# A deeper ring for the down projection's weight tiles: eight places, loads three column pairs ahead

## The chip, the cores and the metric

The kernel runs on one core of a Trainium2 chip, as one launch. The metric is the device time in microseconds, the median of several runs; lower is better. The engines are called by the names that the profile gives them: PE (TensorE), DVE (VectorE), ACT (ScalarE), SP (SyncE, which issues nearly all DMA transfers here). Each engine works through its own queue in order, and the order in every queue is fixed when the kernel is built: a scheduler of the framework simulates the program and, whenever an engine falls free, gives it the ready instruction of the best priority. `tc.high_priority(n)` treats an instruction as if it stood n instructions earlier in the program.

## The reference

One step of a hybrid decoder layer for a prompt (512 tokens behind 16 meta tokens) and eight sample tokens, all in float32 with `D_MODEL` 2048 and `D_FF` 5632: layer norm, one input projection, sliding-window attention beside causal pooling, output projection, layer norm, a SwiGLU feed-forward and a last layer norm. The part that matters here is the end:

```python
def post_sublayers(h, attn_out, pool_out, w_o, ln1_g, ln1_b, w_gate, w_up, w_down, ln2_g, ln2_b):
    mix = jnp.einsum('bte,ed->btd', jnp.concatenate([attn_out, pool_out], -1), w_o)
    h1 = layer_norm(DEEPNORM_ALPHA * h + mix, ln1_g, ln1_b)
    a = jax.nn.silu(jnp.einsum('btd,df->btf', h1, w_gate)) * jnp.einsum('btd,df->btf', h1, w_up)
    ff = jnp.einsum('btf,fd->btd', a, w_down)
    return layer_norm(DEEPNORM_ALPHA * h1 + ff, ln2_g, ln2_b)
```

## The kernel before

**Products.** Each float32 product is made of three matmuls on rounded halves (`products`, lines 188 to 195): high part by high part, high by low, low by high. A weight tile is therefore first split (`split`, lines 181 to 187): ACT casts it into the high part `wh` (line 185), DVE subtracts to get the low part `wl` (line 186). In the down projection `wh` and `wl` have rings of four tiles each, so the cast for a product waits until PE has finished the product four before it. Gate, up and down projections use a seven-product scheme for 2x2 blocks (Strassen's, in Winograd's form): seven block products instead of eight, with some additions of weight tiles (DVE) and of results.

**The down projection** is the stage from about 1470 to 1954 us. Its reduction has 44 tiles of 128. Forty of them go through the seven-product scheme in four chunks `c` of ten (five pairs, `KP = 5`), the other four ("plain", `PLAIN`) through ordinary products in the stage that follows. For each chunk there are eight column pairs `j` (an output tile j and j+8). So the stage works through 32 pairs, `pairs[x]` with x from 0 to 31. `column_pair(c, j)` is a generator that makes the seven products in the order 1, 7, 2, 6, 4, 5, 3, with 5 x 3 = 15 matmuls each. Products 7, 6, 5 and 3 first need an addition of weight tiles in place (`add`, line 1162, 128x640 on DVE, at high priority); results are added from PSUM (`tri`, two sets of three banks) to the accumulators by DVE in lines 1169, 1174, 1179 and 1182, once each per pair. The loop interleaves two pairs: product 1 of pair x, then the last product (3) of pair x-1, then the rest of pair x.

**Loads.** `load_w(c, j)` (lines 1128 to 1141) loads the weights of a pair as two tiles of 640 KB, `r=0` and `r=1`, by SP (line 1135); for the first chunk also the accumulators' start values (line 1141). `A[0, *]` lie in the tile `r=0`, `A[1, *]` in `r=1`. The first addition of a pair, for product 7, writes `A[1, 0]` and needs both tiles. The last read of `r=0` is the split for product 3, which takes `A[0, 1]`; the last read of `r=1` is the split for product 4, which takes `A[1, 1]`. The tiles rotate through the ring `wd`, which has five places of 1280 columns: two and a half pairs. The loop calls `load_w` for the next pair, x+1, after product 3 of pair x-1. `load_ops` (line 1124) loads the other operands of the products, 260 KB each, for the following chunk. The helper `step(sync)` keeps the steps of these loads in SP's queue in program order; within one step the order is free.

**Around it.** The regions `fr`, `rr` and `mid_*` are large SBUF tiles in which the kernel hands out places by column number; the framework makes every load wait for the readers of the bytes that it overwrites. `pl` (line 1245) holds the weights of the plain tiles for four output tiles at a time, 2048 columns; it has one place of its own during the down projection, and a second is added behind it (line 1258). `af` (line 1215) takes the plain activations from `a_d` through two places. After the down projection come the plain products (`down`, lines 1242 to 1255), the transposes and the last layer norm (`Rows`).

Of the kernel before, what the change touches and what calls it, by code (L numbers as in the profile page):

```python
# [7 lines left out]
F32 = mybir.dt.float32  # L8
# [5 lines left out]
P = 128  # L14
# [8 lines left out]
NTOK = NS + SEQ  # L23
# [36 lines left out]
KP = 5  # L60
# [6 lines left out]
def hybrid_step(ctx, tc, xin, w_in, w_o, w_g, w_u, w_d, w_pool, par_d, cst_d, ident_d, ln2gb, kct_d, vc_d, hist_d,  # L67
# [63 lines left out]
    fr, rr = Region("fr", F32, FRW), Region("rr", F32R, RRW)  # L131
# [25 lines left out]
    @contextmanager  # L157
    def step(*engines):

        block = nc.cur_bb.bb  # L160
        last = block.instructions[-1]
        yield
        code = block.instructions
        start = next(k for k in reversed(range(len(code))) if code[k] is last) + 1
        new = {}
        for i in code[start:]:
            if i.engine in [e.engine for e in engines]:
                new.setdefault(i.engine, []).append(i)
                for j in behind.get(i.engine, ()):
                    tc.add_manual_dep(i, j, mybir.DependencyInfo(mybir.DependencyClass.NoSync,  # L170
                                                                 mybir.DependencyReason.DATA), reason="step")
        behind.update({e: [i.name for i in v][-12:] for e, v in new.items()})
# [8 lines left out]
    def split(s, name, lo=None):  # L181

        wh, wl = [sp[0].tile(list(s.shape), F32R, tag=t, bufs=sp[1]) for t in ("wh", "wl")]
        with tc.high_priority(prio[0]):
            nc.scalar.copy(wh, s)  # L185
            (lo or nc.vector).tensor_sub(wl, s, wh.bitcast(F32))  # L186
        return wh, wl
# [56 lines left out]
    with ExitStack() as sa:  # L244
# [235 lines left out]
        for i in range(2):  # L480
            z = zkv[2 + i]
# [311 lines left out]
    pb, gp = Pool(fr), Pool(rr, Region("mid_b", F32R, MDW))  # L793
# [3 lines left out]
    def bank(name, w=HN):  # L797
        return ps.tile([P, 512], F32, tag="bank", name=name, bufs=banks)[:, :w]

    def slot(name, shape=(2, HN), at=None):  # L800
        return gp.tile([P, *shape], F32R, tag="g", name=name, bufs=NG, at=at)
# [268 lines left out]
    for j, s in enumerate(sets[NKEEP:NKEEP + NFILL]):  # L1070
        if j % 2 == 0:
            f = pb.tile([P, 2, HN], F32, tag="fill", name=f"fill{j}", bufs=NF)
# [27 lines left out]
    accp, rp, pb = Pool(fr), Pool(fr), Pool(fr)  # L1100
    low = fr.take(4 * 1280)
    accp.ring("acc", 2 * NTOK, F32, 8)
    up = [fr.take(1280) for _ in range(3)]
    fr.give(low, 4 * 1280)
    rp.rings["wd"] = [[(fr, x) for x in up + [fr.take(1280) for _ in range(2)]], 1280, 0]
    plp = Pool(fr)
    plp.ring("pl", 2048, F32, 1)
    acc4 = []


# [3 lines left out]
    ops, wd, given = [{n: [] for n in ORDER} for _ in range(NCH)], {}, [0]  # L1114

    def load_ops(c, k):

        for n in ORDER:
            while k and len(ops[c][n]) < KP:
                i = WINO[c][len(ops[c][n])]  # L1120
                t = slot(f"op{c}_{n}_{i}", at=free[given[0] % NG])
                given[0] += 1
                with step(sync):
                    nc.sync.dma_start(t.bitcast(F32), t_d[i, {1: 0, 2: 1, 3: 2, 5: 3, 6: 4, 7: 5, 4: 6}[n]])
                ops[c][n].append(t)
                k -= 1

    def load_w(c, j):
        if c == NCH:
            return  # L1130
        with step(sync):
            for r in range(2):
                raw = rp.tile([P, 2 * KP * P], F32, tag="wd", name=f"wd{c}_{j}_{r}", bufs=5)
                o = P * (c % 2)
                nc.sync.dma_start(raw, w_d[c, j + 8 * r, :, o:o + 2 * KP * P])
                v = raw.rearrange("p (k b c) -> p b k c", k=KP, b=2)
                wd[c, j, r, 0], wd[c, j, r, 1] = v[:, 0], v[:, 1]
            if c == 0:
                acc4.append(accp.tile([P, 4, HN], F32, tag="acc", name=f"acc{j}", bufs=8))
                for r in range(2):  # L1140
                    nc.sync.dma_start(acc4[j][:, 2 * r:2 * r + 2, :].rearrange("p a c -> p (a c)"), h1_d[j + 8 - 8 * r])

    def column_pair(c, j):

        A = {(r, b): wd[c, j, r, b] for r in range(2) for b in range(2)}
        tri = ps.tile([P, 3, 512], F32, tag="tri", name=f"tri{c}_{j}", bufs=2)[:, :, :HN]
        ga, de, al = [tri[:, i, :] for i in range(3)]
        ac = acc4[j]
        if c == 0:
            for r in range(2):  # L1150
                h = ac[:, 2 * r:2 * r + 2, :]
                nc.scalar.activation(h, h, AF.Copy, scale=ALPHA)

        def prod(n, bk, src, first=True):
            wh, wl = split(src, f"d{c}_{j}_{n}")
            for k in range(KP):
                hi, lo = ops[c][n][k][:, 0, :], ops[c][n][k][:, 1, :]
                products([bk], wh[:, k, :], wl[:, k, :], [hi], [lo], k == 0 and first, k == KP - 1, True)

        def add(t, a, b, op):  # L1160
            with tc.high_priority(prio[0]):
                op(A[t], A[a], A[b])  # L1162
            return A[t]


        prod(1, al, A[0, 0])
        yield
        prod(7, ga, add((1, 0), (0, 0), (1, 0), nc.vector.tensor_sub))
        nc.vector.tensor_add(ac[:, 1:3, :], ac[:, 1:3, :], tri[:, 0::2, :])
        yield  # L1170
        prod(2, de, A[0, 1])
        yield
        prod(6, al, add((1, 0), (1, 1), (1, 0), nc.vector.tensor_sub), False)
        nc.vector.tensor_add(ac[:, 0, :], ac[:, 0, :], al)
        yield
        prod(4, ga, A[1, 1], False)
        yield
        prod(5, al, add((0, 0), (1, 0), (0, 0), nc.vector.tensor_add), False)
        nc.vector.tensor_add(ac[:, 0:2, :], ac[:, 0:2, :], tri[:, 0::2, :])  # L1179
        yield  # L1180
        prod(3, al, add((0, 1), (0, 1), (1, 0), nc.vector.tensor_sub), False)
        nc.vector.tensor_add(ac[:, 2:4, :], ac[:, 2:4, :], tri[:, 1:3, :])
        yield
# [3 lines left out]
    load_ops(0, 10)  # L1187
    load_w(0, 1)
    load_ops(0, 25)
    pairs = [(c, j) for c in range(NCH) for j in range(8)]  # L1190
    g, before = [column_pair(0, j) for j in range(2)]
    for i in range(6):
        next(g)
        next(before)
    next(g)
    load_w(0, 2)
    for x, (c, j) in enumerate(pairs[2:], 2):
        g = column_pair(c, j)
        next(g)
        next(before)  # L1200
        if x + 1 < len(pairs):
            load_w(*pairs[x + 1])
        for i in range(5):
            next(g)
            if c + 1 < NCH:

                if j < 7 and i == 0:
                    load_ops(c + 1, 3 if c else 5 if j == 6 else 4)
                elif j == 7:
                    load_ops(c + 1, (4, 0, 5, 0, 5)[i])  # L1210
            elif j == 0 and i == 0:

                ah, al_ = [], []
                for f in range(2 * len(PLAIN)):
                    t = pb.tile([P, NTOK], F32, tag="af", name=f"af{f}", bufs=2)
                    with step(sync):
                        nc.sync.dma_start(t, a_d[f])
                    ah.append(slot(f"ah{f}", (NTOK,), 8 + 2 * f))
                    al_.append(slot(f"al{f}", (NTOK,), 9 + 2 * f))
                    nc.scalar.copy(ah[f], t)  # L1220
                    nc.vector.tensor_sub(al_[f], t, ah[f].bitcast(F32))
        before = g
# [4 lines left out]
    scope.close()  # L1227
    ps, banks = ctx.enter_context(tc.tile_pool(name="psD", bufs=8, space=PS)), 8
    rp.close()
    pb.close()  # L1230
    pb, zp = Pool(fr), Pool(Region("mid_c", F32, MDW))
    places = [x for i in PLAIN for x in PLAIN[i]]
    pw, ws = {}, {}
# [8 lines left out]
    def down(h, m):  # L1242

        if m % 4 == 0 and h == 0:
            pw[h] = plp.tile([P, 4, 4, P], F32, tag="pl", name=f"pl{h}_{m}", bufs=len(plp.rings["pl"][0]))
            for f, (c, x) in enumerate(places):
                nc.sync.dma_start(pw[h][:, :, f, :], w_d[c, m:m + 4, :, x * P:(x + 1) * P].rearrange("m p c -> p m c"))
        hs = DHALF[h]
        out = bank(f"d{h}_{m}", hs.stop - hs.start)
        if h == 0:  # L1250
            ws[m] = split(pw[h][:, m % 4], f"dp{m}")
        wh, wl = ws[m]
        for f in range(4):
            products([out], wh[:, f, :], wl[:, f, :], [ah[f][:, hs]], [al_[f][:, hs]], f == 0, f == 3)
        nc.vector.tensor_add(acc[m][:, hs], acc[m][:, hs], out)

    gb = [[pb.tile([P, 512], F32, name=f"gb{i}_{q}") for q in range(4)] for i in range(2)]
    plp.rings["pl"][0].append((fr, fr.take(2048)))
    gb_loads = [(i, q) for i in range(2) for q in range(4)]

    class Rows:
# [124 lines left out]
```

## Time and profile before

| | |
|---|---|
| time, median of 3 runs | 2029.87 us (2023.43 to 2036.59) |
| the profiled execution's own time | 2030.44 us |
| its span, first to last instruction | 2028.7 us |
| mean granted clock of PE | 0.986 |
| busy: PE, DVE, ACT | 95%, 76%, 47% |
| DMA | 319.27 MB, mean 157 GB/s |

How to read it: times are microseconds from the span's start. A matmul counts as busy for about 0.28 us, while in a dense row one starts every 0.12 us, so a busy share of PE hides short stops; the distance between starts shows them. In the timeline a row has the start, the duration, engine, line, operation, output and inputs, and in brackets the idle time in front of it with what ended it. In the list of waits a row says who waited for whom, for how long in total, how often, and the longest. In a table by stretches each engine has its busy time and count of instructions, and the last three columns are PE's granted clock, the DMA share and GB/s.

### The profile page before, as it was taken

What the parts mean: (1) busy time and instruction counts of PE and PEld (TensorE: products, weight loads), DVE (VectorE), ACT (ScalarE), POOL (GpSimd) and SP (SyncE); (2) the same over time, 40 slices, a digit from 0 to 9 for tenths busy, and PEclk for the clock granted to TensorE, in tenths of its full rate; (3) what the DMA queues carried; (4) which work ended last, traced back from release to release, by engine and by line L of the source; (5) the groups of instructions that cost most, each with busy time, mean ns of one, the idle gap of its engine ahead of it and who ended that gap; (6) DMA issues with size and microseconds to landing.
All of it is one profiled execution on the core that took longest, in us unless ns stands there. A gap on an engine that the chain in (4) does not pass through costs nothing.

```text
span 2028.7 us, 39453 instructions
## 1 busy us (share of the span) xinstructions
PE 1934.3 (95%) x15571; PEld 1889.3 (93%) x15571; DVE 1532.7 (76%) x2730; ACT 946.8 (47%) x1805; POOL 2.5 (0%) x8
## 2 busy tenths in 40 slices
PE   8999999999999999999999999999998889898895
PEld 8999999999989999999999999999998888888895
DVE  6665667667678899888888888888776776767768
ACT  6643436445555445555555555555543333333331
POOL 0000000000000000000000000000000000000000
PEclk9999998999999999999999999999999999999998
DMA  8622223665554555454444444445675535453232
GB/s 261 225 94 70 71 80 97 204 199 183 199 176 163 168 178 168 147 166 138 152 147 156 148 149 150 147 158 168 221 285 190 203 126 201 150 190 119 76 89 85
DMA packets 144986, 319.27 MB, mean 157 GB/s; under 512 B 14160, under 2 KB 65944, under 8 KB 144696
## 3 DMA queue, kind: packets, MB, share of 16 engines
q1 hardware_dynamic: 143680, 314.65, 46.5%
q8 instruction: 122, 2.00, 0.4%
q10 hardware_dynamic: 1120, 2.10, 0.3%
q14 instruction: 64, 0.52, 0.1%
HBM read 265.20 MB, written 54.03 MB: 157 GB/s over the span
## 4 chain that ended last, share of the span: by engine, by line
PE 75%; DMA 10%; DVE 9%; issue 3%; ACT 2%; SPq 0%; DVEq 0%; ACTq 0%
PE p_u L195 6%; PE p_u L192 6%; PE p_u L193 6%; DMA fr<-in_w_d_dram 6%; PE p_g L192 5%; PE p_g L193 5%; PE p_g L195 5%; DVE rr L186 4%; PE tri L195 4%; PE tri L192 4%; PE tri L193 3%; PE o L192 3%; PE o L195 3%; PE o L193 3%; DMA fr<-in_w_u_dram 2%
## 5 line engine op out<-in xcount | busy, mean ns | idle before, releaser
L185 ACT CAST rr<-fr 128x512 fp32r<-128x512 f32 (+1 forms) x1056 | 664.3, 643 | 833.0 <-PE tri L193 211.0
L186 DVE TENSOR_TENSOR rr<-fr,rr 128x512 fp32r<-128x512 f32 (+1 forms) x1056 | 733.9, 715 | 203.9 <-ACT rr L185 198.0
L930 DVE TENSOR_TENSOR fr<-fr 128x1024 f32<-128x1024 f32 x176 | 215.1, 1223 | 61.9 <-DMA fr<-in_w_g_dram 31.5
L192 PE MATMUL p_g<-rr 128*128 128x260 f32 x800 | 226.8, 285 | 7.1 <-DVE fr L1001 6.9
L195 PE MATMUL tri<-rr 128*128 128x260 f32 x696 | 202.6, 291 | 28.8 <-DVE rr L186 27.0
L192 PE MATMUL p_u<-rr 128*128 128x260 f32 x800 | 225.8, 283 | 1.8 <-ACT rr L185 1.0
L195 PE MATMUL p_g<-rr 128*128 128x260 f32 x800 | 222.1, 282 | 1.5 <-DVE rr L186 1.5
L195 PE MATMUL p_u<-rr 128*128 128x260 f32 x800 | 222.2, 282 | 0.0
L193 PE MATMUL p_u<-rr 128*128 128x260 f32 x768 | 215.9, 282 | 0.0
L193 PE MATMUL p_g<-rr 128*128 128x260 f32 x768 | 215.8, 282 | 0.0
L192 PE MATMUL tri<-rr 128*128 128x260 f32 x696 | 201.0, 289 | 4.8 <-DVE fr L1179 3.4
L193 PE MATMUL tri<-rr 128*128 128x260 f32 x696 | 199.0, 286 | 0.0
L1162 DVE TENSOR_TENSOR fr<-fr 128x640 f32<-128x640 f32 x128 | 104.5, 821 | 107.3 <-DMA fr<-in_w_d_dram 107.1
L195 PEld LDWEIGHTS tri<-rr 128*128 128x128 f32 x696 | 133.9, 192 | 36.0 <-DVE rr L186 36.0
L192 PEld LDWEIGHTS p_g<-rr 128*128 128x128 f32 x800 | 150.5, 188 | 9.1 <-DVE fr L1001 8.9
L192 PEld LDWEIGHTS p_u<-rr 128*128 128x128 f32 x800 | 150.7, 188 | 2.6 <-ACT rr L185 1.4
L195 PEld LDWEIGHTS p_g<-rr 128*128 128x128 f32 x800 | 149.6, 189 | 1.7 <-DVE rr L186 1.7
L195 PEld LDWEIGHTS p_u<-rr 128*128 128x128 f32 x800 | 149.6, 189 | 0.0
L192 PE MATMUL o<-rr 128*128 128x260 f32 x512 | 146.0, 286 | 0.3 <-ACT rr L185 0.3
L193 PEld LDWEIGHTS p_u<-rr 128*128 128x128 f32 x768 | 144.4, 188 | 0.0
L193 PEld LDWEIGHTS p_g<-rr 128*128 128x128 f32 x768 | 144.3, 188 | 0.0
L195 PE MATMUL o<-rr 128*128 128x260 f32 x512 | 143.9, 283 | 0.2 <-DVE rr L186 0.2
(300 smaller groups left out, 4761.9 us busy)
## 6 DMA issues: line engine op xcount, KB each, us to landing
fr<-in_w_g_dram SPq DMA_DIRECT2D x95, 512.0 KB
fr<-in_w_u_dram SPq DMA_DIRECT2D x95, 512.0 KB
fr<-in_w_d_dram SPq DMA_DIRECT2D x64, 640.0 KB
t_d<-fr SPq DMA_DIRECT2D x140, 260.0 KB
fr<-in_w_o_dram SPq DMA_DIRECT2D x64, 512.0 KB
fr<-in_w_in_dram SPq DMA_DIRECT2D x46, 512.0 KB
rr<-t_d SPq DMA_DIRECT2D x87, 260.0 KB
mid_b<-t_d SPq DMA_DIRECT2D x53, 260.0 KB
```

What stands on the lines that cost most here:

```text
L185: nc.scalar.copy(wh, s)
L186: (lo or nc.vector).tensor_sub(wl, s, wh.bitcast(F32))
L192: nc.tensor.matmul(o, wh, hi[j], start=first, stop=False, skip_group_check=onto)
L193: nc.tensor.matmul(o, wh, lo[j], start=False, stop=False, skip_group_check=onto)
L195: nc.tensor.matmul(o, wl, hi[j], start=False, stop=last, skip_group_check=onto)
L930: op(self.q(*t), self.q(*a), self.q(*b))
L1162: op(A[t], A[a], A[b])
```

## The change

The ring `wd` gets eight places, four pairs. `load_w` for pairs 2 and 3 is called before the first pairs start, for pair 4 after them, and in the loop for pair x+3 instead of x+1. To make room, three other things move. The plain weights have no place during the down projection; after it their two places are laid over the first two and the fifth and sixth place of the ring. The plain activations `af` are loaded into four places of the operand ring (slots 16 to 19) instead of two of their own. The places that the plain weights take are cut out of the free list, so that the last layer norm's factors `gb` go elsewhere.

```diff
-    up = [fr.take(1280) for _ in range(3)]
+    up = [fr.take(1280) for _ in range(4)]
     fr.give(low, 4 * 1280)
-    rp.rings["wd"] = [[(fr, x) for x in up + [fr.take(1280) for _ in range(2)]], 1280, 0]
-    plp = Pool(fr)
-    plp.ring("pl", 2048, F32, 1)
+    rp.rings["wd"] = [[(fr, x) for x in up + [fr.take(1280) for _ in range(4)]], 1280, 0]
...
-                raw = rp.tile([P, 2 * KP * P], F32, tag="wd", name=f"wd{c}_{j}_{r}", bufs=5)
+                raw = rp.tile([P, 2 * KP * P], F32, tag="wd", name=f"wd{c}_{j}_{r}", bufs=8)
...
     load_w(0, 1)
     load_ops(0, 25)
+    load_w(0, 2)
+    load_w(0, 3)
...
     next(g)
-    load_w(0, 2)
+    load_w(0, 4)
     for x, (c, j) in enumerate(pairs[2:], 2):
         g = column_pair(c, j)
         next(g)
         next(before)
-        if x + 1 < len(pairs):
-            load_w(*pairs[x + 1])
+        if x + 3 < len(pairs):
+            load_w(*pairs[x + 3])
...
-                    t = pb.tile([P, NTOK], F32, tag="af", name=f"af{f}", bufs=2)
+                    t = slot(f"af{f}", (NTOK,), 16 + f).bitcast(F32)
...
     rp.close()
+    plp = Pool(fr)
+    plp.rings["pl"] = [[(fr, x[0]) for x in (up, [0])], 2048, 0]
+    for x in up[0], 0:
+        fr.spare = [z for y in fr.spare for z in ((y[0], min(y[1], x)), (max(y[0], x + 2048), y[1])) if z[0] < z[1]]
...
-            pw[h] = plp.tile([P, 4, 4, P], F32, tag="pl", name=f"pl{h}_{m}", bufs=len(plp.rings["pl"][0]))
+            pw[h] = plp.tile([P, 4, 4, P], F32, tag="pl", name=f"pl{h}_{m}", bufs=2)
...
-    plp.rings["pl"][0].append((fr, fr.take(2048)))
```

## The prediction

> **What bounds the kernel now.** I read the page first: its span, the busy row, the chain, and the group of the additions in the down projection.
>
> ```profile
> span 2028.7 us, 39453 instructions
> PE 1934.3 (95%) x15571; PEld 1889.3 (93%) x15571; DVE 1532.7 (76%) x2730; ACT 946.8 (47%) x1805; POOL 2.5 (0%) x8
> PE 75%; DMA 10%; DVE 9%; issue 3%; ACT 2%; SPq 0%; DVEq 0%; ACTq 0%
> L1162 DVE TENSOR_TENSOR fr<-fr 128x640 f32<-128x640 f32 x128 | 104.5, 821 | 107.3 <-DMA fr<-in_w_d_dram 107.1
> ```
>
> TensorE is the bound, and a tenth of the chain is DMA, most of it the loads of `w_d`. VectorE sits 107.1 us before the additions of line 1162 until such a load lands. Next, the waits between 1470 and 1954 us (the down projection), the stretch from the third pair to the thirtieth, a stretch of the up projection beside it, and the one-per-pair instruction of line 1174 at both ends of the first stretch.
>
> ```profile
> DVE fr L1162 <- DMA fr<-in_w_d_dram: 105.6, 28, 5.5
> PE tri L195 <- DVE rr L186: 34.2, 26, 2.6
> 1507.40:1911.90 404.50, 362.51 (x2837) 350.27 (x2835) 284.92 (x409) 142.24 (x200) 0.00 (x0) 0.98 0.46 162
> 800.00:900.00 100.00, 99.48 (x828) 99.07 (x827) 85.14 (x136) 50.87 (x97) 0.00 (x0) 1.00 0.46 151
> 1507.38 0.42 DVE L1174 TENSOR_TENSOR fr<-fr,tri 128x260 f32<-128x260 f32 x1 [1.48 <-PE tri L195]
> 1911.94 0.42 DVE L1174 TENSOR_TENSOR fr<-fr,tri 128x260 f32<-128x260 f32 x1
> ```
>
> The two L1174 rows are 27 pairs apart: (1911.94 - 1507.38) / 27 = 14.98 us for a pair. A pair is 7 products of 15 matmuls. In the up projection 828 matmuls take 100 us, 0.121 us each, so 105 would take 12.7 us. The lost time is 27 x 2.3 = 62 us. VectorE works 284.92 / 27 = 10.6 us per pair and DMA 0.46 of the time: neither is full. The whole question is whether this change removes the VectorE wait.
>
> One period, queue by queue (SP issues, VectorE, ScalarE, TensorE):
>
> ```profile
> 1735.16 0.33 SPq L1135 DMA_DIRECT2D fr<-in_w_d_dram  x1
> 1735.58 1.33 SPq L1124 DMA_DIRECT2D rr<-t_d  x3
> 1732.38 1.55 DVE L186 TENSOR_TENSOR rr<-fr,rr 128x640 fp32r<-128x640 f32 x2
> 1734.30 0.83 DVE L186 TENSOR_TENSOR rr<-fr,rr 128x640 fp32r<-128x640 f32 x1
> 1739.11 0.83 DVE L1162 TENSOR_TENSOR fr<-fr 128x640 f32<-128x640 f32 x1 [3.98 <-DMA fr<-in_w_d_dram]
> 1739.85 0.82 DVE L186 TENSOR_TENSOR rr<-fr,rr 128x640 fp32r<-128x640 f32 x1
> 1737.56 0.73 ACT L185 CAST rr<-fr 128x640 fp32r<-128x640 f32 x1 [3.29 <-PE tri L193]
> 1739.39 0.28 PE L193 MATMUL tri<-rr 128*128 128x260 f32 x1
> 1740.72 0.39 PE L195 MATMUL tri<-rr 128*128 128x260 f32 x1 [1.05 <-DVE rr L186]
> ```
>
> The L186 that starts at 1734.30 is a pair's last read of its `r=0` tile (product 3). It ends at 1735.13, call this the hand-over, and SP issues the waiting load at 1735.16. VectorE stands before an addition until the load has landed, 3.98 us later. Behind it is the L186 that TensorE needs: its ScalarE cast ended at 1738.29, it could have run then, and it runs at 1739.85. TensorE stops for 1.33 - 0.12 = 1.2 us. A four-microsecond load thus costs over a microsecond per pair, because an addition stands ahead of more urgent work in an in-order queue.
>
> **Whose addition is it?** The last additions of the stage tell:
>
> ```profile
> 1918.38 0.82 DVE L1162 TENSOR_TENSOR fr<-fr 128x640 f32<-128x640 f32 x1 [5.15 <-DMA fr<-in_w_d_dram]
> 1920.46 0.82 DVE L1162 TENSOR_TENSOR fr<-fr 128x640 f32<-128x640 f32 x1
> 1921.93 0.82 DVE L1162 TENSOR_TENSOR fr<-fr 128x640 f32<-128x640 f32 x1
> 1923.84 0.82 DVE L1162 TENSOR_TENSOR fr<-fr 128x640 f32<-128x640 f32 x1
> 1932.93 0.82 DVE L186 TENSOR_TENSOR rr<-fr,rr 128x640 fp32r<-128x640 f32 x1 [2.76 <-ACT rr L185]
> 1933.79 0.82 DVE L1162 TENSOR_TENSOR fr<-fr 128x640 f32<-128x640 f32 x1
> 1935.88 0.82 DVE L1162 TENSOR_TENSOR fr<-fr 128x640 f32<-128x640 f32 x1
> 1937.95 0.82 DVE L1162 TENSOR_TENSOR fr<-fr 128x640 f32<-128x640 f32 x1
> ```
>
> A pair has four additions (products 7, 6, 5, 3). Around the last pair there are three, so its first one, for product 7, is the one that waited at 1918.38. The waiting addition belongs to the pair after the one in work, and its result is wanted only by the L186 at 1932.93, 14 us later. Nothing forces it there. The queue order is fixed when the kernel is built, and an addition is put where its load is expected to land. How far ahead? The stage's first pair says:
>
> ```profile
> 1404.73 0.33 SPq L1135 DMA_DIRECT2D fr<-in_w_d_dram  x1
> 1412.66 0.82 DVE L1162 TENSOR_TENSOR fr<-fr 128x640 f32<-128x640 f32 x1
> 1469.69 0.39 PE L192 MATMUL tri<-rr 128*128 128x260 f32 x1 [0.76 <-ACT rr L185]
> ```
>
> Its addition ran 8 us after the load was issued and 57 us before the stage's first matmul. Distance doesn't hold an addition back: three pairs are 38 us.
>
> **The change, part by part.** No matmul, cast, subtraction, addition or byte of `w_d` is added. What moves:
>
> *Ring of eight, three pairs ahead.* Eight places are four pairs. In the iteration of pair x, `load_w(x+3)` takes the places of pair x-1, whose `r=0` tile is released by the same L186 as now (1734.30). Today `r=1` of x+1 goes onto `r=0` of x-1: the gating load leaves at the same hand-over. The weights are now 38 us early for their use, but the first addition of pair x+3 can be put exactly where that of x+1 stands, in the hole between the hand-over and the urgent L186 (2.76 us in row 1932.93, with no load pending). If so, the wait is still 4.0 us and TensorE's loss is unchanged: 0 us on the steady pairs. Only its size could differ: the companion tile (`r=1`) is released by product 4's L186, about 2 us earlier (1732.38), so its transfer is over before `r=0` starts. Bounds: 0 if it is clear; if it is in the way, one tile at the rate of this row, 655 KB / 405 GB/s = 1.6 us per pair.
>
> ```profile
> 1886.00:1888.10 2.10, 2.10 (x20) 2.10 (x19) 0.03 (x1) 0.75 (x2) 0.00 (x0) 1.00 1.00 405
> 1920.00 0.59 PE L195 MATMUL tri<-rr 128*128 128x260 f32 x1 [2.25 <-DVE rr L186]
> 1938.18 0.36 PE L192 MATMUL tri<-rr 128*128 128x260 f32 x1 [0.55 <-DVE fr L1169]
> 1501.95 0.39 PE L192 MATMUL tri<-mid_b,rr 128*128 128x260 f32 x1 [1.97 <-DVE fr L1169]
> 1953.65 5.63 SPq L1247 DMA_DIRECT2D fr<-in_w_d_dram  x8
> ```
>
> SP's queue: both loads wait at the point where one does now, and the loads of `t_d` behind them (1735.58) keep their times.
>
> *The end.* The last load leaves three hand-overs before the end instead of one, so the last two waits go. They cost 1.2 us, as in the period above, and 2.4 us (row 1920.00: 2.25 + 0.28 - 0.12), plus about 1.3 us of slow matmuls behind that longer gap. About 0.7 us remains of each for other reasons (row 1938.18): 4.9 - 1.4 = 3.5 us saved.
>
> *The start.* `load_w(0,2)` and `(0,3)` now follow the first 25 operand loads, without waiting for pair 0. TensorE's 2.1 us stop at 1501.95, when pair 2 was late, should go; but the hand-overs of pairs 0 and 1 now carry loads of pairs 4 and 5, at 1.2 us each if both bite. I take 1 us saved; bounds -3 to +4 (both waits against the whole stop and its slow matmuls).
>
> *Plain weights and `af`.* The first plain tile loses its place of its own and loads after pair 28, some 38 us before its use; the second loads after pair 30. Cover: three pairs of matmuls. Were it gone, four loads of 256 KB at 405 GB/s would cost 2.6 us. The loads at 1953.65 stay behind the first tile's reads. The four `a_d` loads no longer share two places. I take 0.5 us saved, bounds -2 to +4.
>
> Sum: 0 + 3.5 + 1 + 0.5 = 5 us. The profiled execution took 2030.4 us (span 2028.7 and 1.7 around it; the median is 2029.9): **2025 us**. With those bounds this case reaches from 2012 to 2036.
>
> **The rivals.**
>
> *The wait goes.* The slot found at build depends on the expected landing. At the chunk borders, where the load has other transfers before it, the addition already stands behind the urgent L186:
>
> ```profile
> 1708.29 0.83 DVE L186 TENSOR_TENSOR rr<-fr,rr 128x640 fp32r<-128x640 f32 x1 [3.15 <-ACT rr L185]
> 1710.81 1.56 DVE L1162 TENSOR_TENSOR fr<-fr 128x640 f32<-128x640 f32 x2 [1.69 <-DMA fr<-in_w_d_dram]
> ```
>
> If the pair of loads is expected a little later than the single one now, all additions slide behind it, and most of the 62 us goes. Leaving 0.3 us per pair (half of row 1938.18) gives 62 - 8 + 5 = 59 us: 1971 us; 1962 to 1985. For it: VectorE has 2 us to spare per pair. Against it: the same hand-over, the same hole. The Trainium skill (Perfetto Trace Analysis, Identifying Performance Opportunities) says that a gap which repeats on the engine that should be full can mean too little SBUF for the next tile; by that rule this deeper ring is the cure and the time is this rival's. The repeating gap is here, but its row shows a queue's order as well as a full ring. Chance 0.21. A mixture, with only some chunks freed, 1985 to 2012: 0.09.
>
> *Slower: both tiles leave at the hand-over, `r=0` first.* Then the gating landing is 1.6 us later, with the addition still in the hole: 27 x 1.6 = 43 us, 2068 us. It decides as soon as `r=1` goes second. Longer stops also bring slow matmuls, as here, where starts go from 0.12 to 0.21 us apart:
>
> ```profile
> 1831.22 0.59 PE L192 MATMUL tri<-rr 128*128 128x260 f32 x1 [2.54 <-DVE fr L1179]
> 1831.61 0.42 PE L193 MATMUL tri<-rr 128*128 128x260 f32 x1
> 1831.82 0.42 PE L195 MATMUL tri<-rr 128*128 128x260 f32 x1
> ```
>
> At 1.3 us per pair that would add 35 us: 2103 us. The Trainium skill (TensorE: Matmul & The Clock Gate, What's actually happening) puts the fall to half clock after an idle window of about 3.4 us; by it the price would stay at 2068. The gap here was 2.54 + 0.28 = 2.8 us and the matmuls did slow, so the row is taken. Against the rival: `r=1` is free first. Chance 0.11.
>
> **How the numbers follow.** Forecast 0.59, wait goes 0.21, mixture 0.09, slower 0.11. 1% (20 us) is about what a measurement here can tell from no change. Faster by over 1%: 0.21 + 0.08 + 0.02 of the forecast's edge = 0.31; slower 0.11; within 1% 0.58. The range goes down to 1965, into the case where the wait goes, and up to 2040, which leaves out most of the slower case.
>
> **What would show it.** Right: line 1162 still waits some 100 us for `w_d`, about 4 us at a time, pairs stay near 15 us, and the last two hand-overs are free. Wrong: that wait is near zero and pairs take under 13.2 us (the wait goes), or it is over 5 us at a time (slower). What makes me wrong is the slot that the additions get in VectorE's queue.

## The result, and the profile after

The changed kernel takes 2040.53 us (median of 16 runs, 2036.85 to 2048.12) against 2029.57 us for the kernel before beside it: ratio 1.006, interval 1.0045 to 1.0075. The forecast was 2025 us with a range of 1965 to 2040: the time lies half a microsecond beyond the range, and on the other side of the old time than was forecast. The effect is small, 0.6%. The profiled execution took 2042.2 us.

The page of the changed kernel: span, busy row, chain, and the group of the additions (line 1160 is the old 1162; lines behind 1107 have moved up by two).

```profile
span 2040.4 us, 39488 instructions
PE 1939.2 (95%) x15571; PEld 1896.8 (93%) x15571; DVE 1534.8 (75%) x2730; ACT 946.6 (46%) x1805; POOL 2.5 (0%) x8
PE 71%; DVE 12%; DMA 11%; issue 3%; ACT 2%; DVEq 0%; SPq 0%; ACTq 0%
L1160 DVE TENSOR_TENSOR fr<-fr 128x640 f32<-128x640 f32 x128 | 104.8, 822 | 102.5 <-DMA fr<-in_w_d_dram 102.3
```

The wait for `w_d` that the change aimed at is still 102.3 us (107.1 before), and VectorE's share of the chain rose from 9% to 12%. The list of waits of the down projection (1470 to 1960 us) and the table for the stretch from the third pair to the thirtieth:

```profile
DVE fr L1160 <- DMA fr<-in_w_d_dram: 102.3, 24, 5.6
PE tri L195 <- DVE rr L186: 41.0, 22, 2.8
```

```profile
1505.66:1929.82 424.16, 370.91 (x2837) 360.93 (x2836) 287.85 (x409) 141.74 (x199) 0.00 (x0) 0.95 0.46 153
```

The 27 pairs took 404.56 us before (1911.94 - 1507.38) and take 424.16 now, with the same 2837 matmuls in the two tables. TensorE waits 41.0 us for the low-part subtraction instead of 34.2, and its granted clock over the stretch is 0.95 instead of 0.98. The instruction once per pair (old 1174, now 1172), in the timeline:

```profile
1505.66 0.43 DVE L1172 TENSOR_TENSOR fr<-fr,tri 128x260 f32<-128x260 f32 x1 [1.60 <-PE tri L195]
1929.82 0.43 DVE L1172 TENSOR_TENSOR fr<-fr,tri 128x260 f32<-128x260 f32 x1 [0.30 <-PE tri L195]
1956.56 0.43 DVE L1172 TENSOR_TENSOR fr<-fr,tri 128x260 f32<-128x260 f32 x1 [0.29 <-PE tri L195]
```

So the difference of the spans, 11.7 us, splits like this (each part lies between two such rows, or between a row and an end of the span):

| part | before | after | difference | forecast |
|---|---|---|---|---|
| up to the first pair's row | 1480.74 | 1480.19 | -0.6 | 0 |
| first to third pair | 26.64 | 25.47 | -1.2 | -1 |
| 27 steady pairs | 404.56 | 424.16 | **+19.6** | 0 |
| last two pairs | 30.12 | 26.74 | -3.4 | -3.5 |
| behind the last pair | 86.6 | 83.8 | -2.8 | -0.5 |

A steady pair takes 15.71 us instead of 14.98; in four other kernels below that keep the queue's order but have no whole companion in front of the load it takes 14.87 to 15.10, so 0.73 us is well beyond the spread. What differs inside a pair is seen in two neighbouring periods of the timeline: SP's two loads, VectorE's addition with the subtraction behind it, TensorE's stop.

```profile
1723.98 0.33 SPq L1133 DMA_DIRECT2D fr<-in_w_d_dram  x1
1725.89 0.33 SPq L1133 DMA_DIRECT2D fr<-in_w_d_dram  x1
1731.00 0.83 DVE L1160 TENSOR_TENSOR fr<-fr 128x640 f32<-128x640 f32 x1 [5.14 <-DMA fr<-in_w_d_dram]
1731.74 0.82 DVE L186 TENSOR_TENSOR rr<-fr,rr 128x640 fp32r<-128x640 f32 x1
1732.61 0.39 PE L195 MATMUL tri<-rr 128*128 128x260 f32 x1 [2.20 <-DVE rr L186]
1740.01 0.33 SPq L1133 DMA_DIRECT2D fr<-in_w_d_dram  x1
1742.89 0.33 SPq L1133 DMA_DIRECT2D fr<-in_w_d_dram  x1
1746.96 0.82 DVE L1160 TENSOR_TENSOR fr<-fr 128x640 f32<-128x640 f32 x1 [4.10 <-DMA fr<-in_w_d_dram]
1747.70 0.82 DVE L186 TENSOR_TENSOR rr<-fr,rr 128x640 fp32r<-128x640 f32 x1
1748.57 0.38 PE L195 MATMUL tri<-rr 128*128 128x260 f32 x1 [1.62 <-DVE rr L186]
```

The first load of each couple is `r=1`, the second the gating `r=0`. From the second load to the addition: 1731.00 - 1725.89 = 5.1 us where `r=1` left 1.9 us ahead, 1746.96 - 1742.89 = 4.1 us where it left 2.9 us ahead. Over the stage, in the pairs whose addition stands ahead of the urgent subtraction, the second load took 4.5 to 5.6 us to the addition (mean 5.1, 12 pairs) where `r=1` had left less than 2 us ahead, and 3.9 to 4.4 us where it had left 2.8 to 2.9 us ahead (six of seven pairs; the other took 5.3). Of the 24 waits 10 last 4.9 us or more, the longest 5.6; before the change 2 of 28 did.

The table by stretches tells how much of `r=1` was still to come when `r=0` left, here from the first load to the second of each couple above:

```profile
1723.98:1725.89 1.91, 1.72 (x14) 1.51 (x14) 1.87 (x3) 0.73 (x1) 0.00 (x0) 1.00 0.51 91
1740.01:1742.89 2.88, 2.88 (x27) 2.88 (x26) 2.08 (x3) 0.99 (x2) 0.00 (x0) 1.00 0.64 214
```

In the first 91 GB/s x 1.91 us = 0.17 MB had moved, in the second 214 x 2.88 = 0.62 MB, of a tile of 0.66 MB. With a lead of 1.9 us three quarters of the companion were still in front of the gating load, with 2.9 us nearly nothing. A longer stop costs twice, as TensorE's starts show:

```profile
1905.21 0.28 PE L193 MATMUL tri<-rr 128*128 128x260 f32 x1
1907.64 0.39 PE L195 MATMUL tri<-rr 128*128 128x260 f32 x1 [2.14 <-DVE rr L186]
1908.19 0.42 PE L195 MATMUL tri<-rr 128*128 128x260 f32 x1
1908.40 0.42 PE L192 MATMUL tri<-rr 128*128 128x260 f32 x1
```

2.43 us without a start, then starts 0.21 us apart instead of 0.12. The granted clock (the third figure from the end) fell to 0.50 there, for 3.4 us, and was 1.00 on both sides:

```profile
1904.57:1907.98 3.41, 1.27 (x10) 1.06 (x9) 1.96 (x3) 0.73 (x1) 0.00 (x0) 1.00 0.04 17
1907.98:1911.39 3.41, 3.41 (x18) 3.41 (x17) 3.21 (x6) 1.46 (x2) 0.00 (x0) 0.50 0.00 0
1911.39:1914.80 3.41, 3.41 (x31) 3.41 (x30) 3.34 (x5) 0.98 (x2) 0.00 (x0) 1.00 0.02 5
```

Summed over the matmul starts of the 27 steady pairs, what distances over 0.3 us hold beyond 0.12 us grew from 50.7 to 61.1 us, and the same for distances of 0.15 to 0.3 us from 13.5 to 23.1 us: 10.4 and 9.6 us, together the whole of the 19.6 us within the accuracy of such sums.

### The profile page after: what moved, and what is told of

It reads as the page before. It is cut to its first block, busy times and chain, and to the rows that moved or that the text cites. A ratio compares the mean times of both kernels' runs of the same rounds, so it can differ in the third digit from the quotient of the medians.

```text
span 2040.4 us, 39488 instructions
## 1 busy us (share of the span) xinstructions
PE 1939.2 (95%) x15571; PEld 1896.8 (93%) x15571; DVE 1534.8 (75%) x2730; ACT 946.6 (46%) x1805; POOL 2.5 (0%) x8
## 4 chain that ended last, share of the span: by engine, by line
PE 71%; DVE 12%; DMA 11%; issue 3%; ACT 2%; DVEq 0%; SPq 0%; ACTq 0%
DMA fr<-in_w_d_dram 6%; PE p_u L195 6%; PE p_u L192 6%; PE p_u L193 6%; DVE rr L186 5%; PE p_g L192 5%; PE p_g L193 5%; PE p_g L195 5%; PE tri L192 4%; PE tri L195 4%; PE tri L193 4%; PE o L192 3%; PE o L195 3%; PE o L193 3%; DMA fr<-in_w_u_dram 2%
## 5 line engine op out<-in xcount | busy, mean ns | idle before, releaser
L195 PE MATMUL tri<-rr 128*128 128x260 f32 x696 | 205.9, 296 | 37.4 <-DVE rr L186 36.3
L192 PE MATMUL tri<-rr 128*128 128x260 f32 x696 | 204.4, 294 | 4.9 <-DVE fr L1177 1.8
L193 PE MATMUL tri<-rr 128*128 128x260 f32 x696 | 202.7, 291 | 0.0
L1160 DVE TENSOR_TENSOR fr<-fr 128x640 f32<-128x640 f32 x128 | 104.8, 822 | 102.5 <-DMA fr<-in_w_d_dram 102.3
```

The costliest lines, as they stand in the source:

```text
L192: nc.tensor.matmul(o, wh, hi[j], start=first, stop=False, skip_group_check=onto)
L193: nc.tensor.matmul(o, wh, lo[j], start=False, stop=False, skip_group_check=onto)
L195: nc.tensor.matmul(o, wl, hi[j], start=False, stop=last, skip_group_check=onto)
```

## The experiments

**The theory**: an addition for a later pair stands in VectorE's in-order queue ahead of an urgent subtraction and waits there for its load, whatever the ring's depth; the change added only the companion `r=1` in front of that load. **Rivals**: the ring was too shallow; three pairs ahead or the ring's place costs by itself; the bytes in the way are not what lengthens the wait.

**1. The changed kernel with the addition behind its own pair's subtraction.** In `split` the low-part subtraction is remembered, and the addition of product 7 is issued after that of product 1. No data, load or wait on data changes.

```diff
+    low_sub = [None]
...
-            (lo or nc.vector).tensor_sub(wl, s, wh.bitcast(F32))
+            low_sub[0] = (lo or nc.vector).tensor_sub(wl, s, wh.bitcast(F32)).ins
...
         prod(1, al, A[0, 0])
+        first = low_sub[0]
         yield
-        prod(7, ga, add((1, 0), (0, 0), (1, 0), nc.vector.tensor_sub))
+        with tc.issue_after(first):
+            seven = add((1, 0), (0, 0), (1, 0), nc.vector.tensor_sub)
+        prod(7, ga, seven)
```

> The changed kernel with one ordering added: the addition for product 7 of a pair is queued on VectorE behind the pair's own first low-part subtraction (product 1), so it can no longer stand three pairs early. Loads, ring and places are those of the changed kernel. Queue-order theory: the wait of the additions on w_d (102 us in the changed kernel) falls to under 5 us, and a pair takes what the last three pairs of the changed kernel take without a load in front of them, 13.4 us instead of 15.7: 26 x 2.3 = 60 us less, 1980 us (1972 to 1992). Rival, the loads themselves are the limit (landing or ring too short): the wait moves to another reader of the tiles and the time stays at 2035 to 2045.

Measured 1982.36 us, ratio 0.9774 (0.9754 to 0.9794). Its timeline (all lines below `split` are two further down):

```profile
1652.52 0.33 SPq L1135 DMA_DIRECT2D fr<-in_w_d_dram  x1
1655.28 0.82 DVE L188 TENSOR_TENSOR rr<-fr,rr 128x640 fp32r<-128x640 f32 x1 [2.79 <-ACT rr L187]
1656.14 0.82 DVE L1162 TENSOR_TENSOR fr<-fr 128x640 f32<-128x640 f32 x1
```

The load still leaves at the hand-over, but no addition waits for it: VectorE waits only for ScalarE's cast. A pair takes 13.54 us ((1864.09 - 1498.60) / 27, by the sum of line 1172, once a pair). The queue's order is the cause of the wait.

**2. The kernel before with the same order.** The same edit on the ring of five.

> The kernel before (ring of five, loads one pair ahead) with the same ordering on VectorE and nothing else. Queue-order theory: a load that lands 4 us after the hand-over is some 10 us early for the addition where it is now, so depth is not needed: 27 x (14.98 - 13.4) = 43 us less than before, 1986 us (1975 to 1998), within 15 us of the changed kernel with the ordering. Rival, the ring of five is too short: the wait stays above 50 us in total and the time above 2010 us, and only the deep ring with the ordering is fast.

Measured 1984.22 us, ratio 0.9782 (0.9765 to 0.98), 13.43 us per pair, level with the first run. With five places and one pair ahead the largest wait for `w_d` in the down projection is

```profile
ACT rr L187 <- DMA fr<-in_w_d_dram: 12.3, 3, 8.0
```

and 11.7 of the 12.3 us lie behind the last pair. The old ring was deep enough.

**3. Seven places, two pairs ahead.** With an odd number of places the gating load leaves with no companion ahead of it, as in the kernel before. (Not shown: the loads before the loop are one pair fewer, and the plain weights lie over the third, fifth and sixth place.)

```diff
-    rp.rings["wd"] = [[(fr, x) for x in up + [fr.take(1280) for _ in range(4)]], 1280, 0]
+    rp.rings["wd"] = [[(fr, x) for x in up + [fr.take(1280) for _ in range(3)]], 1280, 0]
...
-        if x + 3 < len(pairs):
-            load_w(*pairs[x + 3])
+        if x + 2 < len(pairs):
+            load_w(*pairs[x + 2])
```

> The changed kernel with seven places and loads two pairs ahead, plain weights over the third place and the fifth and sixth. With an odd ring the tile r=0 finds its place free a pair earlier, and only r=1 leaves at the hand-over, alone, as in the kernel before. Companion theory (in the changed kernel the gating load lands 4 to 5.6 us after its issue because its companion left only 2 to 3 us ahead of it): waits return to 3.8 us on average, a steady pair to 15.0 us, and the time is 2040 - 26 x 0.75 = 2021 us (2014 to 2028). Rival (the later landing comes from the new places, the new loop position or the plain weights): waits of 4.3 us on average stay and the time is 2035 to 2045.

Measured 2019.93 us, ratio 0.9966 (0.9951 to 0.9981).

```profile
DVE fr L1160 <- DMA fr<-in_w_d_dram: 98.4, 26, 5.6
```

One of the 26 waits is over 4.9 us, and a pair takes (1905.33 - 1501.73) / 27 = 14.95 us: the 14.98 of before. Without the companion ahead the loss is gone, with the wait still in place. This run changes the ring and the lead as well; runs 5 and 6 hold both.

**4. Each tile's load in a step of its own, `r=0` first.** (The loads of the accumulators' start values get a step of their own behind them, not shown.)

```diff
-        with step(sync):
-            for r in range(2):
+        for r in range(2):
+            with step(sync):
```

> The changed kernel with the two tiles of a pair in separate steps of SP's queue, r=0 before r=1, so that both leave at the hand-over and r=1 lands last. In VectorE's queue of this kernel the addition for product 7 of pair x+3 stands behind the urgent subtraction of product 7 of pair x, or further back, not ahead of it. Queue-order theory: although the load lands later (5.5 to 6 us after the hand-over), its wait no longer holds up the urgent subtraction; waits fall to 1 to 2.5 us each and the time to 1985 to 2015 us. Rival (what counts is when the load lands): each wait grows by 1 us or more and the time is 2055 to 2075 us.

Measured 2005.86 us, ratio 0.9892 (0.9871 to 0.9913), 14.30 us per pair. The additions now stand behind the urgent subtraction, as in this stretch:

```profile
1705.89 0.81 SPq L1133 DMA_DIRECT2D fr<-in_w_d_dram  x2
1709.00 0.82 DVE L186 TENSOR_TENSOR rr<-fr,rr 128x640 fp32r<-128x640 f32 x1 [3.14 <-ACT rr L185]
1709.86 0.83 DVE L1161 TENSOR_TENSOR fr<-fr 128x640 f32<-128x640 f32 x1
```

And the list of waits:

```profile
DVE fr L1161 <- DMA fr<-in_w_d_dram: 3.1, 4, 1.6
PE tri L192 <- DVE fr L1168: 32.3, 26, 2.1
```

The addition needs both tiles, and the later one, now `r=1`, leaves behind `r=0` at the hand-over; still the wait for `w_d` falls to 3.1 us. What is left is a sum (line 1168) that comes late, 32.3 us. A pair of loads expected later helped, because the additions moved with it.

**5 and 6. The size of the companion.** Ring and loop are those of the changed kernel, and so is VectorE's queue in the steady pairs; only the bytes of `r=1` differ. At the chunk borders the queue was laid out anew: there the addition of product 7 stands behind the urgent subtraction in the changed kernel, ahead of it in these two.

```diff
-                nc.sync.dma_start(raw, w_d[c, j + 8 * r, :, o:o + 2 * KP * P])
+                h = KP * P if r and len(wd) > 16 else 2 * KP * P
+                nc.sync.dma_start(raw[:, :h], w_d[c, j + 8 * r, :, o:o + h])
```

(with `P` in the place of the first `KP * P` in run 6).

> The ring of eight as changed, but from the fifth pair on only the first half of each r=1 tile is loaded (the rest keeps old weights, so the result is not the reference's). VectorE's queue order is that of the changed kernel. Companion theory (the r=1 transfer, in flight when the gating r=0 load leaves, delays its landing): half of it is out of the way sooner, the mean wait of the hoisted addition falls from 4.26 us to 3.8-4.0 us, the pair from 15.71 us to 15.0-15.3 us, 2029 us (2020 to 2035). Rival (the longer pairs come from loading three ahead or from where the ring lies, not from the companion's bytes): pairs stay at 15.7 us, 2040 us (2036 to 2046).

> As the run with half companions, but only a tenth of each r=1 tile is loaded (64 KB of 640). VectorE's queue order is that of the changed kernel. Companion theory: wait 3.7-3.8 us as before the change, the pair 14.9-15.0 us, and with the start, end and tail of the changed kernel kept 2020 us (2014 to 2027); the 14.98 us per pair of the kernel before come back, no less, as the addition still stands ahead of the urgent subtraction. Rival (three ahead, or the ring's place): 2040 us (2036 to 2046). A second rival (all of SP's issues of w_d matter, and fewer bytes relieve everything): well under 2010 us.

Measured: half, 2026.94 us, ratio 0.9991 (0.9967 to 1.0015), 14.99 us per pair; a tenth, 2017.64 us, ratio 0.9945 (0.9919 to 0.997), 14.87 us per pair. The times are where the companion theory put them, and the pairs 0.01 and 0.03 us under its ranges; the mean waits are not there: 109.8 / 25 = 4.4 and 106.5 / 25 = 4.3 us, no shorter than in the changed kernel. The mean was a poor indicator: short waits of 0.5 to 1.6 us at the chunk borders pull the changed kernel's down, and these two have none. The count of waits of 4.9 us or more tells it: 10 with the whole companion, 4 with half, 2 with a tenth. Half a companion, from the timeline of run 5:

```profile
1609.45 0.33 SPq L1134 DMA_DIRECT2D fr<-in_w_d_dram  x1
1611.39 0.33 SPq L1134 DMA_DIRECT2D fr<-in_w_d_dram  x1
1615.92 0.83 DVE L1161 TENSOR_TENSOR fr<-fr 128x640 f32<-128x640 f32 x1 [4.55 <-DMA fr<-in_w_d_dram]
1624.47 0.33 SPq L1134 DMA_DIRECT2D fr<-in_w_d_dram  x1
1626.42 0.33 SPq L1134 DMA_DIRECT2D fr<-in_w_d_dram  x1
1630.49 0.82 DVE L1161 TENSOR_TENSOR fr<-fr 128x640 f32<-128x640 f32 x1 [4.10 <-DMA fr<-in_w_d_dram]
```

It left 1.9 us ahead, like the whole one at 1723.98, and the gating load took 4.5 and 4.1 us instead of 5.1. Over the stage 20 gating loads had half a companion less than 2 us ahead: they took 3.9 to 5.6 us, 4.4 on average, against 5.1 behind a whole one.

**7. Eight places, but two pairs ahead in the loop.** `load_w(*pairs[x + 2])`, one pair less before the loop.

> The ring of eight, but the loop loads two column pairs ahead instead of three: the places of the load were read a whole pair earlier, so it needs no hand-over. In VectorE's queue the addition of the pair after next still stands ahead of the urgent subtraction in most pairs. Theory (the wait is the time from hand-over to landing; a load that needs no hand-over leaves earlier): the addition finds its weights there, its wait falls from 102 us to under 25 us, pairs take 13.4-14.2 us, 1990 us (1980 to 2008). Rival (SP's in-order queue keeps the load at the same moment, or the addition is put just as much too early before its landing): wait stays near 90 us, 2020 us (2012 to 2042).

Measured 2033.21 us, ratio 1.0011 (0.9993 to 1.0029): my theory missed by 43 us, the rival held. The waits of SP and of VectorE, and one period of the timeline:

```profile
SPq L1133 <- DVE rr L186: 242.2, 43, 14.2
DVE fr L1160 <- DMA fr<-in_w_d_dram: 85.3, 21, 6.0
```

```profile
1718.83 0.33 SPq L1133 DMA_DIRECT2D fr<-in_w_d_dram  x1
1720.52 0.82 DVE L186 TENSOR_TENSOR rr<-fr,rr 128x640 fp32r<-128x640 f32 x1
1721.37 0.33 SPq L1133 DMA_DIRECT2D fr<-in_w_d_dram  x1
1725.61 0.83 DVE L1160 TENSOR_TENSOR fr<-fr 128x640 f32<-128x640 f32 x1 [4.26 <-DMA fr<-in_w_d_dram]
```

The gating load leaves 0.03 us after the hand-over ended, exactly as with three ahead. In the built program the loads of pair 12 wait for the subtractions of pair 8 in both kernels: SP runs ahead of the loop and fills a place as soon as it is free. **With eight places, it is the number of places that sets when a load leaves; two or three pairs of lead in the loop make no difference.** That a full ring loads at a hand-over at any depth follows by argument; it was run with five, seven and eight places. This kernel lost less per pair (15.33 us): 17 of its waits are over 3 us, against 21 in the changed kernel. Why its queue came out so was not tested.

**8 and 9. One more order.** In run 1 TensorE still waited at each product 6 for the sum that reads product 7's bank, behind the addition of product 5. That addition goes behind the sum:

```diff
-        nc.vector.tensor_add(ac[:, 1:3, :], ac[:, 1:3, :], tri[:, 0::2, :])
+        sums = nc.vector.tensor_add(ac[:, 1:3, :], ac[:, 1:3, :], tri[:, 0::2, :]).ins
...
-        prod(5, al, add((0, 0), (1, 0), (0, 0), nc.vector.tensor_add), False)
+        with tc.issue_after(sums):
+            five = add((0, 0), (1, 0), (0, 0), nc.vector.tensor_add)
+        prod(5, al, five, False)
```

> The changed kernel with the order of the first run (the addition of product 7 behind the low-part subtraction of product 1), and the addition of product 5 put behind the sum that reads the banks of product 7. In the first run TensorE waited for that sum 27 times, 0.55 us before each product 6. If the addition ahead of it in VectorE's queue is what makes it late: 0.3-0.5 us per pair less, 1971 us (1966 to 1978). If the sum waits for TensorE itself, or the subtraction of product 6 is late in its place: 1982 us (1978 to 1990).

> The kernel before (ring of five, one pair ahead, plain weights in places of their own) with both orders of the last run: the addition of product 7 behind the low-part subtraction of product 1, the addition of product 5 behind the sum that reads the banks of product 7. If the deeper ring is worth nothing once the queue is in order: 1974 us (1968 to 1981), level with the 1972 us of the changed kernel with both orders. If the deeper ring helps once the additions no longer stand in the way: over 1982 us.

Measured: on the changed kernel 1972.13 us, ratio 0.9713 (0.9669 to 0.9757), on the kernel before 1975.42 us, ratio 0.9744 (0.9724 to 0.9764); their intervals overlap. The wait of run 1 and the same of run 8:

```profile
PE tri L194 <- DVE fr L1172: 16.0, 27, 1.1
```

```profile
PE tri L194 <- DVE fr L1172: 0.9, 1, 0.9
```

It is gone, and a pair takes 13.16 us (13.20 in run 9). Both beat both kernels of this case by some 55 to 70 us. The 3 us between them can't be told from nothing by the times; in the profiles the stretch behind the last pair is 83.9 us in run 8 and 86.7 in run 9, so most of it goes with the plain weights (run 10) and not with the ring.

**10. The plain weights alone.** The kernel before with the plain tiles over the ring's places, the edit of `plp` from the change and nothing else.

> The kernel before with only the last part of the change: the two plain weight tiles take the ring's places at its end instead of places of their own (ring of five, one pair ahead, the a_d tiles as before). If the plain weights' place is what shortened the stretch behind the last pair by 2.8 us (the casts that wait 11.6 us there for weights wait 5.5 us): that stretch 84 us, the pair 15.0 us, 2027 us (2022 to 2032). If that gain comes from the a_d tiles or the ring: the stretch stays at 86.6 us, 2030 us (2026 to 2034). The times can hardly tell these apart, the stretch in the profile can.

Measured 2025.8 us, ratio 0.9985 (0.9967 to 1.0003), which can't be told from no change. The casts that wait for weights behind the last pair, in the kernel before, the changed one and this one:

```profile
ACT rr L185 <- DMA fr<-in_w_d_dram: 11.6, 2, 8.3
```

```profile
ACT rr L185 <- DMA fr<-in_w_d_dram: 5.5, 1, 5.5
```

```profile
ACT rr L185 <- DMA fr<-in_w_d_dram: 6.0, 2, 5.6
```

The stretch behind the last pair is 2029.4 - 1944.71 = 84.7 us: 2 of the 2.8 us come with the plain weights' place. (It is 86.6 to 86.7 us in the three kernels that keep the old places, 83.8 to 84.3 in those with the whole change.) A pair takes 15.10 us here, against 14.98 in the kernel before with the same ring.

## Why the prediction was wrong, step by step

- **Whose addition waits, and that it keeps its slot: right.** Three pairs ahead the addition went into the same hole, 102.3 us of waits against the forecast's "some 100 us". Runs 1 and 2 show that this order costs some 45 us and that depth isn't needed to be rid of it; the prediction priced a queue in order at 59 us, and it takes the second order of runs 8 and 9 to come near (54 to 57). The Trainium skill (Perfetto Trace Analysis, Identifying Performance Opportunities) reads a repeating gap as a possible lack of SBUF: here more SBUF for the ring made 0.6% more time, and another order in the old SBUF 2.2% less.
- **"The gating load leaves at the same hand-over": right.** Run 7 shows that it couldn't be otherwise while the ring is kept full.
- **"Its transfer is over before `r=0` starts" (0 us): this is the term that failed.** Forecast 0, bounds 0 to 1.6 us per pair; measured 15.71 - 14.98 = 0.73 us, 19.6 us in all, and runs 3, 5 and 6 take it away by taking the companion or its bytes away. I compared a 2 us lead with 1.6 us of bytes at the full rate. The row for it was in the prediction: a load of this size took 4 us from issue to landing, so one that left 1.9 us ahead is still under way (0.17 of its 0.66 MB had moved). I also left the upper bound, 27 x 1.6 = 43 us, out of that case's own range (2012 to 2036) and put it on the rival only. The bounds that I did give for the start and the plain weights reach from 2019 to 2032; the rest of that range has no reason in the prediction.
- **The rival on the slower side: its price was in part real, its condition not.** `r=1` does leave first; nearly half of its 1.6 us per pair was paid all the same. Where `r=0` goes first (run 4) the kernel became faster, as the additions moved behind the subtraction. The rival held the queue fixed while its load moved; the queue is laid out anew at each build.
- **Slow matmuls behind longer stops: right in kind.** The granted clock of the steady pairs fell from 0.98 to 0.95. The Trainium skill (TensorE: Matmul & The Clock Gate, What's actually happening) puts the fall behind an idle window of about 3.4 us; here it came after 2.43 us without a start, so the measurement decides. A limit for the length of a stop isn't shown: in the same stage a stop of 2.77 us, from 1620.2, passed without a fall.
- **The end, -3.5 against -3.4: right.** The last wait for `w_d` now ends at 1906.02, two pairs earlier, and in the last two pairs TensorE is at most 0.8 us without a start (2.5 before).
- **The start, -1 against -1.2: the number by luck.** I said that TensorE's stop at 1501.95 came from the late pair 2 and should go. It is still there:

```profile
1500.26 0.36 PE L192 MATMUL tri<-mid_b,rr 128*128 128x260 f32 x1 [1.78 <-DVE fr L1167]
```

Line 1167 is the old 1169, the same sum; before the change the stop was 1.97 us. VectorE works without a wait for a load in front of that sum in both kernels. Where the other microsecond comes from was not traced.
- **Plain weights, -0.5 against -2.8: too small**, within its bounds (up to 4 saved). I priced the transfers that the new place would add, and overlooked that a cast already waited 8.3 us there for weights whose place was late.

With the two terms as measured the forecast's own sum is 2025 + 20 - 2 = 2043 us; the profiled execution took 2042.2. As both terms were measured in that execution, this says only that the sum lacks no other large term.

## What to carry to other kernels

When an engine waits for a load, ask first whose operand it is and what stands behind the waiting instruction: if it is for later work, move it in the queue before buying depth. A ring that is kept full loads at a hand-over, here with five places as with eight, so more places put the load further from its use, but no further from an instruction that was placed right behind its landing. Price a second transfer in front of a gating one by issue to landing, not by bytes over the full rate.

## What the runs showed of the hardware

A 640 KB load took 4.3 us on average from issue to the addition that waits for it when another of 640 KB had left 2.8 to 2.9 us ahead (7 loads, 3.9 to 5.3), and 5.1 us when that had left less than 2 us ahead (12 loads, 4.5 to 5.6); behind 320 KB at the same lead it took 4.4 us (20 loads, 3.9 to 5.6). Half the bytes in front thus removed the whole loss per pair (14.99 us against 15.71 and, with 64 KB, 14.87): what counts is the part of the companion still to come, 0.49 of 0.66 MB in the row above with the lead of 1.9 us, 0.04 in the one with 2.9. And the longer stops cost twice: over the 27 pairs 10 us more without starts, and 10 us more in slow matmuls, which come in stretches of 3.4 us (one of 6.8) at a granted clock of 0.50.
